# Weight sums of four stages' first units made in device memory ahead of time

## The chip, the cores and the metric

One core of one Trainium2 chip runs the whole program. The metric is the device time of one execution in microseconds (us); the time of a kernel is the median of its runs. For one execution there is a profile: which engine ran which instruction when, what each wait was released by, and what the sixteen DMA engines moved. Engines are named as the profile names them: PE multiplies matrices (PEld loads its weights), DVE and ACT work on elements, POOL is used here almost only to issue accumulating transfers, SP issues plain transfers.

## The reference

One layer of a streaming encoder on 512 frames of width 2048, all in 32-bit floats:

```python
h = rms_norm(x, norm_mix_w);  proj = h @ w_in        # split into two groups
y_a = banded softmax attention (16 heads);  y_g = gated linear attention (4 heads), norm, silu gate
x = x + concat([y_a, y_g]) @ w_out
u = causal_depthwise_conv(rms_norm(x, norm_ffn_w) @ w_ffn_up, w_ffn_conv, b_ffn_conv)
x = x + (gelu(u_gate) * u_val) @ w_ffn_down          # inner width 5632
x = x + sigmoid(rms_norm(x, norm_ple_w) @ w_ple_gate) * (p @ w_ple_proj)
return rms_norm(x, final_norm_w)
```

## The kernel before

The program has two halves. **The first**, up to some 320 us, projects values for the linear attention (`vproj`, lines 230 to 258: sixteen weight pages of 128 x 1024, two column halves of eight), then does the linear attention head by head (`gla_proj`, line 1110, and `gla_core`, line 1158), then projects values for the softmax attention (`values_a`, line 1036). A weight page comes by `wtile` (line 116): one DMA on SP into one of three raw pages, a rounded copy by ACT, the remainder by DVE, each into one of three pages more. In the second half of the value projection `input_pair` (line 1067) also writes the operands of the next stage to memory, seven pieces of 128 KB for each of eight pairs (line 276, all issued by SP).

**The second** is a list of stages, each a matrix product done by Winograd's form of the 2 x 2 block product: a unit is a pair of output blocks, and takes seven products of 24 matmuls (`product`, line 481) from seven weight pages: L11, L12, L22 are blocks of the weights, and S1 = L21 + L22, S2 = S1 + L11, S3 = L21 + L11, S4 = S2 + L12 are sums of blocks. The order of the products is P1, P2, P6, P5, P7, P3, P4, with pages L11, L12, S2, S1, S3, S4, L22. Stages run in the order `pp`, `in` (query, key and gate projections with softmax attention beside them), `pp`, `wo`, `up`, `dn0`, `dn1`, `dn2`, `pg`. In `wo`, `up`, `dn0` to `dn2` and `pg` the first two and the last two units run as pairs, product by product in turn.

How a unit gets its sums is set by a word, `sums`. For `"dma"`, the word of the first and last pairs of all stages here, SP loads L21 into two pages (line 406) and POOL adds L22 to the one and L11 to the other by accumulating DMAs (line 407), which gives S1 and S3; DVE makes S2 into a page of its own (line 431) and turns it into S4 in place (line 440). Pages come from a pool of nine (`free`, line 376), in the order of the list `wanted` (built on line 852 from `NEEDS`); `issue` (line 389) starts a load whenever a page is free, `used` (line 409) frees a page after its last use. Two steps before a product, `prep_high` makes sums and has ACT round the page (line 465); `prep_low` has DVE take the remainder (line 472). At a stage's start ACT and DVE also split the stage's operands, read back from memory (`load` on line 336 and `split` on line 342; the last two pieces come straight from the units before).

The order of the work has two sources. From the stages on, DVE, ACT and PE keep the program's order (`InOrder`, line 56, switched on at line 1277), and a hand-written `agenda` says at which step what is done. Everything else, and SP and POOL throughout, is ordered by the framework's scheduler when the program is built; each engine then runs its list strictly in that order, waiting where an instruction's inputs aren't there.

Of the kernel before, what the change touches and what calls it, by code (L numbers as in the profile page):

```python
# [12 lines left out]
ALU = mybir.AluOpType  # L13

P = 128
# [16 lines left out]
PLAIN = ("P1", "P2", "P6", "P5", "P7", "P3", "P4")  # L32
HALVES = ("P1", "P2", "P6", "P7", "P4", "P5", "P3")
# [8 lines left out]
def encoder_block(ctx: ExitStack, tc: tile.TileContext, A, out):  # L42
    nc = tc.nc
# [4 lines left out]
    pg = ctx.enter_context(tc.tile_pool(name="pages", bufs=1))  # L48
# [54 lines left out]
    late = []  # L103
# [107 lines left out]
    nmix, nffn, nple, nfin = (cols[:, i * KD:(i + 1) * KD] for i in range(4))  # L211
# [4 lines left out]
    first = xslot(0, "x0_0")  # L216
# [50 lines left out]
    def scratch(name, shape):  # L267
        return dp.tile(list(shape), F32, name=name)
# [36 lines left out]
    mixd = operand_scratch("mix", 8)  # L305
# [7 lines left out]

    class Stage:
        def __init__(self, name, units, kb, xd, weights, after, sums, edge, last=PLAIN, begin=None, begin_at=0,
                     chained=False, pace=None, late=(), single=False):
            self.name, self.kb, self.xd, self.weights, self.after = name, kb, xd, weights, after
            self.begin, self.begin_at, self.pace, self.late = begin, begin_at, pace, late
            self.chained, self.tail, self.quarter = chained, [None, None], None
            self.n = (4, kb - 4 - 2 * chained)  # L320
            self.x = {}
            n = len(units)
            self.units = [Unit(self, u, last if i >= n - 2 else PLAIN, edge if i < 2 or i >= n - 2 else sums)
                          for i, u in enumerate(units)]
            for i in range(n):
                self.units[i].pos = i
            if single:
                self.groups = [[u] for u in self.units]
                return
            self.units[0].first = True  # L330
            for i in range(2):
                self.units[i].head = i
                self.units[n - 2 + i].last = i
            self.groups = [self.units[:2]] + [[u] for u in self.units[2:-2]] + [self.units[-2:]]
# [7 lines left out]
        def split(self, op, g, body=True, tails=(0, 1)):  # L342
# [6 lines left out]
            if self.chained and g == 1:  # L349
# [4 lines left out]


    NEEDS = {"dma": ("L11", "L12", "S1", "S2*", "S3", "L22"), "dve": ("L11", "L12", "L21", "L22", "S1*", "S2*"),
             "s3": ("L11", "L12", "L21", "L22", "S1*", "S2*")}

    class Unit:
        def __init__(self, stage, u, order, sums):  # L360
            self.stage, self.u, self.order, self.sums = stage, u, order, sums
            self.first, self.head, self.last = False, None, None
            self.w, self.tag = {}, {}
            if sums == "dma":
                self.uses = dict(L11=2, L12=2, S1=2, S2=2, S3=1, L22=1)
                self.made = {"S2", "S4"}
            else:
                self.uses = dict(L11=3, L12=2, S1=2, S2=2, L21=2, L22=2)
                self.made = {"S1", "S2", "S3", "S4"}
            self.parts = dict(C11=2, C12=2, C22=2, C21=1)  # L370
            self.have = set()
            self.left = dict(A=4, B=1, C=2)
            self.o = None
            self.banks = {}
# [14 lines left out]
    def issue():  # L389
        kept, i = 0, 0  # L390
        while i < len(wanted):
            unit, name = wanted[i]
            if len(free) <= kept:
                return
            if name[-1] == "*":
                kept += 1
                i += 1
                continue
            wanted.pop(i)
            n = unit.stage.kb * P  # L400
            t = raw_page(unit, name)[:, :n]
            src = lambda q: unit.stage.weights(unit.u, q)
            if name[0] == "L":
                nc.sync.dma_start(t, src(name))
            else:
                nc.sync.dma_start(t, src("L21"))
                nc.gpsimd.dma_start(t, src("L22" if name == "S1" else "L11"), accum_op=ALU.add)  # L407

    def used(unit, name):
        unit.uses[name] -= 1  # L410
# [35 lines left out]
    def prep_high(i, own=None):  # L446
        if i >= len(steps):
            return None
        unit, prod = steps[i]
        name = PRODUCTS[prod][0]  # L450
        n = unit.stage.kb * P
        make(unit, name)
        if prod == unit.order[0] and unit.sums != "dma":
            make(unit, "S1")
        if i + 1 < len(steps):
            nxt, p = steps[i + 1]
            q = PRODUCTS[p][0]
            if (nxt is unit or nxt.paired) and (q != "S4" or "P6" in nxt.w):
                make(nxt, q)
        if i > 0 and steps[i - 1][1] == "P6" and steps[i - 1][0].paired:  # L460
            make(steps[i - 1][0], "S4")
        key = {"S4": "S2"}.get(name, "L21" if name == "S3" and unit.sums != "dma" else name)
        raw = unit.w[key]
        hi, lo = own or (page("wh", "wh", F32R), page("wl", "wl", F32R))
        act.activation(hi[:, :n], raw[:, :n], AF.Copy)
        unit.w[prod] = hi, lo
        return unit, key, hi[:, :n], lo[:, :n], raw[:, :n]
# [61 lines left out]
    streams = [x_in] + [scratch(f"x{i}d", (8, P, 2, T)) for i in range(1, 4)]  # L529
    h2d, h3d = operand_scratch("h2", 8), operand_scratch("h3", 8)  # L530
# [112 lines left out]
    def after_gate(unit):  # L643
# [5 lines left out]
                (3, 0, lambda: nc.sync.dma_start(x3d[unit.u], xs))] + squares(unit, 2)  # L649

    blk2 = lambda w: lambda m, q: w[m + 8 * (q[1] == "2"), int(q[2]) - 1]
    stages = [Stage("wo", list(range(8)), 8, mixd, blk2(A["w_out"]), after_norm(streams[1], h2d, nffn), "s3", "dma",
                    begin=lambda u: load_x(streams[0], u), begin_at=6, chained=True)]
    order, f0, slots = [], 0, {}
    for ci, n in enumerate(CHUNKS):
        for k in range(n // 2):
            for second in range(2):
                f = f0 + k + second * n // 2
# [1 line left out]
                slots[f] = (ci, k, second)  # L660
        f0 += n
    stages.append(Stage("up", order, 8, h2d, lambda f, q: A["w_up"][f + FB * (q[1] == "2"), int(q[2]) - 1], after_up,
                        "dma", "dma", chained=True, pace=(22, 5.8), late={-3: 2, -2: 6, -1: 12}))
    stages[0].quarter = last_quarter(lambda: stages[4], nffn)
    for u in stages[1].units:
        u.slot = slots[u.u]
# [163 lines left out]
    mids = streams[1:3] + [scratch("x2d_", (8, P, 2, T)), streams[3]]  # L830
    for ci, n in enumerate(CHUNKS):
        stages.append(Stage(f"dn{ci}", list(range(8)), n // 2, gd[ci], blk2(A[f"w_dn{ci}"]),
                            after_add(mids[ci + 1]) if ci < 2 else after_norm(streams[3], h3d, nple),
                            "dve", "dma", begin=lambda u, s=mids[ci]: load_x(s, u), begin_at=0 if ci else 8, late={}))
    stages.append(Stage("pg", list(range(8)), 8, h3d, blk2(A["w_ple_gate"]), after_gate, "dma", "dma", last=HALVES,
                        begin=load_gate, begin_at=9, chained=True, pace=(15, 5.3), late={}))
    stages[4].quarter = last_quarter(lambda: stages[8], nple)

    stages[0].tail = tails
# [65 lines left out]
    def more_banks():  # L905
        aux_tags[:] = ["b6", "b7"]
        banks.extend(("b4", "b5"))

    agenda[base[front.units[7]] + 7 + 12].append((5, attention_done))
    agenda[i0 + 9].append((0, more_banks))  # L910
    for st in stages:
# [124 lines left out]
    def values_a(c, between=None, then=None):  # L1036
        def place(t):
            vstage[c, t] = xslot(4 * c + t, "va")
            return vstage[c, t]

        vproj(A["w_v_a"], c, place, between=between, then=then)
        for t in range(TT):
            (nc.scalar if c else nc.sync).dma_start(vad[4 * c:4 * c + 4, :, t].rearrange("b p v -> p b v"),
                              vstage[c, t].rearrange("p (b v) -> p b v", b=4))
# [3 lines left out]
    with ExitStack() as mix:  # L1048
        vp = mix.enter_context(tc.tile_pool(name="v", bufs=1, side="right"))

        with ExitStack() as gctx:
# [106 lines left out]
            def gla_core(hd, eb, en, dd, dec2):  # L1158
# [60 lines left out]
                for vb in range(2):  # L1219
                    nc.vector.scalar_tensor_tensor(o[vb], o[vb], gnw[:, vb:vb + 1], rg, ALU.mult, ALU.mult)  # L1220
                    nc.sync.dma_start(ond[hd][:, vb], o[vb])

            st = gla_proj(0)
            for hd in range(1, 4):
                nxt = gla_proj(hd)
                gla_core(hd - 1, *st)
                st = nxt
            values_a(0)
            gla_core(3, *st)

    xa.append(ctx.enter_context(tc.tile_pool(name="xa", bufs=1, side="right", reuse_waits="tile")))
# [283 lines left out]
```

## Time and profile before

| | us |
|---|---|
| median of 3 runs | 2297.38 |
| lowest, highest | 2296.74, 2305.6 |
| the profiled execution | 2290.98 |
| its span, from the first to the last instruction | 2289.3 |

The page of the profile gives the busy time of each engine, the DMA queues (q1 is fed by SP, q0 by POOL) and the chain of work that ended last. Beside it the trace answers questions: the timeline of one engine in a stretch, the busy times of all engines in chosen stretches, groups of like instructions. A row of a timeline reads: start, duration, engine, line, operation, what is written from what, count, and in brackets the idle time before it with what ended it. L64 is the helper behind `vec`, `act` and `ten`, so there the names of the tiles tell the rows apart: `wh` and `wl` are the rounded page and the remainder, `l` a loaded weight page, `s` a page of sums, `wo_R`, `up_R` and so on operands, `acc` accumulators.

### The profile page before, as it was taken

Reading aid. Unit: us, or ns where it says so; the run is one execution under the profiler, and the core shown is the slowest. Engines: PE = TensorE matmul, PEld = TensorE weight load, DVE = VectorE, ACT = ScalarE, POOL = GpSimd, SP = SyncE. Lnnn points to the kernel's source line nnn. Section 1 sums busy time; section 2 is a strip of 40 time slices with the busy share of each in tenths; the row PEclk is TensorE's granted clock in tenths of the full one; section 3 lists DMA queues with packets and bytes.
Section 4 is the critical chain, followed back from the end, with each engine's and each line's share of the span. In section 5 each row is a group of like instructions: output and inputs, shape, how many; then the busy total and the mean of one; then the engine's idle time right before and its main releaser. Section 6 shows DMA issues by size and latency. Waiting matters only on the chain.

```text
span 2289.3 us, 44978 instructions
## 1 busy us (share of the span) xinstructions
PE 2255.1 (99%) x18004; PEld 2183.3 (95%) x18004; DVE 1885.3 (82%) x2587; ACT 1302.1 (57%) x1913; POOL 143.6 (6%) x181
## 2 busy tenths in 40 slices
PE   9999999999999999999999999999999999999997
PEld 8888889999999999999999999999999999999997
DVE  7566369998788888998888888888898787998987
ACT  6354357776665665555555555555564554656656
POOL 0000000000000100000000000010000100001000
PEclk9999999999999999999999999999999999999998
DMA  6623596666978977787877777777866967879895
GB/s 218 206 74 104 179 283 171 184 183 200 316 252 258 326 215 212 203 223 205 222 199 222 213 216 208 216 212 214 254 212 230 314 219 241 300 242 330 273 289 191
DMA packets 195570, 516.78 MB, mean 226 GB/s; under 512 B 20928, under 2 KB 72384, under 8 KB 195360
## 3 DMA queue, kind: packets, MB, share of 16 engines
q1 hardware_dynamic: 167168, 423.42, 52.8%
q0 software_dynamic: 23616, 84.95, 21.1%
q10 hardware_dynamic: 4576, 5.54, 0.7%
q8 instruction: 141, 2.31, 0.4%
q14 instruction: 69, 0.57, 0.1%
HBM read 435.18 MB, written 76.55 MB: 224 GB/s over the span
## 4 chain that ended last, share of the span: by engine, by line
PE 84%; DVE 7%; DMA 4%; ACT 3%; issue 2%; ACTq 0%; DVEq 0%; SPq 0%; POOLq 0%
PE accA L64 39%; PE accC L64 20%; PE accB L64 10%; PE v L252 3%; PE v L254 3%; PE v L253 3%; DVE wl L64 2%; DMA l<-in_w_dn 1%; DVE s L64 1%; DMA s<-in_w_dn 1%; PE py L64 1%; PE ptr L64 1%; PE psc L64 1%; DMA wo_T<-mix_T 1%; DMA s<-in_w_blk 1%
## 5 line engine op out<-in xcount | busy, mean ns | idle before, releaser
L64 DVE TENSOR_TENSOR wl<-s,wh 128x1024 fp32r<-128x1024 f32 (+1 forms) x365 | 437.5, 1199 | 62.8 <-ACT wh L64 61.7
L64 ACT ACTIVATE wh<-l 128x1024 fp32r<-128x1024 f32 (+1 forms) x308 | 319.2, 1037 | 184.8 <-PE accC L64 117.2
L64 DVE TENSOR_TENSOR wl<-l,wh 128x1024 fp32r<-128x1024 f32 (+1 forms) x308 | 367.6, 1194 | 56.8 <-ACT wh L64 56.4
L64 ACT ACTIVATE wh<-s 128x1024 fp32r<-128x1024 f32 (+1 forms) x365 | 377.9, 1036 | 34.8 <-DVE s L64 18.5
L64 ACT ACTIVATE u<-accA 128x256 f32<-128x256 f32 x290 | 109.4, 377 | 363.8 <-PE accA L64 363.7
L64 DVE TENSOR_TENSOR s<-s,l 128x1024 f32<-128x1024 f32 (+1 forms) x192 | 229.5, 1195 | 9.4 <-DMA s<-in_w_blk 9.2
L64 PE MATMUL accA<-up_T,wh 128*128 128x256 f32 x1408 | 178.9, 279 | 0.1
L64 PEld LDWEIGHTS accA<-up_T,wh 128*128 128x128 f32 x1408 | 170.6, 188 | 0.3 <-ACT wh L64 0.3
L64 DVE SCALAR_TENSOR_TENSOR cv<-u,cw,cv 128x511 f32<-128x511 f32 (+1 forms) x176 | 131.5, 747 | 3.1
L407 POOL DMA_DIRECT2D s<-in_w_up x88 | 75.1, 853 | 788.3 <-DMA s<-in_w_up 360.6
L252 PE MATMUL v<-wv_h,h 128*128 128x512 f32 x256 | 100.2, 391 | 0.4 <-ACT h L153 0.4
L254 PE MATMUL v<-wv_h,h 128*128 128x512 f32 x256 | 100.2, 391 | 0.0
L253 PE MATMUL v<-wv_l,h 128*128 128x512 f32 x256 | 99.7, 389 | 0.0
L64 PE MATMUL accA<-up_T,wl 128*128 128x256 f32 x704 | 96.5, 279 | 0.0
L64 PE MATMUL accB<-up_R,wh 128*128 128x256 f32 x704 | 90.5, 280 | 2.0 <-DVE up_R L64 1.3
L64 PE MATMUL accA<-dn_T,wh 128*128 128x256 f32 x704 | 90.4, 280 | 1.9 <-ACT wh L64 1.9
L64 PE MATMUL accA<-up_R,wh 128*128 128x256 f32 x704 | 89.7, 279 | 0.0
L64 PE MATMUL accC<-up_N,wh 128*128 128x256 f32 x704 | 89.3, 279 | 0.0
L64 PE MATMUL accC<-up_R,wh 128*128 128x256 f32 x704 | 89.3, 279 | 0.0
L64 PE MATMUL accA<-up_N,wh 128*128 128x256 f32 x704 | 89.3, 279 | 0.0
L64 PEld LDWEIGHTS accA<-up_T,wl 128*128 128x128 f32 x704 | 88.5, 188 | 0.0
L64 PEld LDWEIGHTS accB<-up_R,wh 128*128 128x128 f32 x704 | 85.7, 188 | 2.7 <-DVE up_R L64 1.5
(402 smaller groups left out, 5060.0 us busy)
## 6 DMA issues: line engine op xcount, KB each, us to landing
l<-in_w_up SPq DMA_DIRECT2D x132, 512.0 KB, 5.4
s<-in_w_up SPq DMA_DIRECT2D x88, 512.0 KB, 4.7
s<-in_w_up POOLq DMA_DIRECT2D x88, 512.0 KB, 6.3
l<-in_w_dn SPq DMA_DIRECT2D x56, 448.0 KB, 5.2
l<-in_w_blk SPq DMA_DIRECT2D x36, 512.0 KB, 4.5
l<-in_w_out SPq DMA_DIRECT2D x28, 512.0 KB, 4.9
l<-in_w_dn SPq DMA_DIRECT2D x28, 512.0 KB, 5.6
s<-in_w_blk SPq DMA_DIRECT2D x24, 512.0 KB, 4.6
```

What stands on the lines that cost most here:

```text
L64: ins = f(*args, **kw)
L252: nc.tensor.matmul(ps[t], h1[kt][:, 0, sl], wh, start=kt == 0, stop=False)
L253: nc.tensor.matmul(ps[t], h1[kt][:, 0, sl], wl, start=False, stop=False)
L254: nc.tensor.matmul(ps[t], h1[kt][:, 1, sl], wh, start=False, stop=kt == KD - 1)
L407: nc.gpsimd.dma_start(t, src("L22" if name == "S1" else "L11"), accum_op=ALU.add)
```

## The change

A third word, `"memory"`, for the first two units of `wo`, `up`, `dn0` and `pg`: eight units. For each, four pages in device memory (rows of 1152 floats apart, 1024 used) take the sums. `sum_begin` copies L21 into two of them, L11 and L12 into the others, by plain DMAs on SP from memory to memory; `sum_add` then makes S1 (+ L22), S3 (+ L11), S2 (+ S1) and S4 (+ S2) by accumulating DMAs on POOL from memory to memory. The calls for six units stand between the heads of the linear attention, those for the two of `pg` at five steps of the stage `in`. When the stages come, all seven pages of such a unit are loaded as they are by SP, each into a page of its own that is free again after one use. The unit then needs no addition on DVE and no accumulating DMA. All other units are as before.

```diff
+            how = [first or edge] * 2 + [sums] * (n - 4) + [edge] * 2
...
+             "memory": ("L11", "L12", "S2", "S1", "S3", "S4", "L22"),
...
+            if sums == "memory":
+                self.uses = dict.fromkeys(NEEDS[sums], 1)
+                self.made = set()
...
             if name[0] == "L":
                 nc.sync.dma_start(t, src(name))
+            elif unit.sums == "memory":
+                nc.sync.dma_start(t, sumd[unit, name])
...
+    def sum_begin(unit):
+        src = lambda q: unit.stage.weights(unit.u, q)
+        for name, q in (("S1", "L21"), ("S3", "L21"), ("S2", "L11"), ("S4", "L12")):
+            sumd[unit, name] = scratch(f"{unit.stage.name}{unit.u}_{name}", (P, 1152))[:, :unit.stage.kb * P]
+            nc.sync.dma_start(sumd[unit, name], src(q))
+
+    def sum_add(unit, *names):
+        for name in names:
+            q = {"S1": "L22", "S3": "L11", "S2": "S1", "S4": "S2"}[name]
+            nc.gpsimd.dma_start(sumd[unit, name], sumd[unit, q] if q[0] == "S" else unit.stage.weights(unit.u, q),
+                                accum_op=ALU.add)
+
+    def sum_step(us, i):
+        if i < len(us):
+            sum_begin(us[i])
+        for back, names in ((1, ("S1", "S3")), (2, ("S2",)), (3, ("S4",))):
+            if 0 <= i - back < len(us):
+                sum_add(us[i - back], *names)
...
+    for i in range(5):
+        agenda[base[front.units[2 + i]]].append((0, lambda i=i: sum_step(summed[6:], i)))
...
+            sum_step(summed[:6], 0)
             st = gla_proj(0)
+            sum_step(summed[:6], 1)
             for hd in range(1, 4):
                 nxt = gla_proj(hd)
+                sum_step(summed[:6], 2 * hd)
                 gla_core(hd - 1, *st)
+                sum_step(summed[:6], 2 * hd + 1)
                 st = nxt
             values_a(0)
+            sum_step(summed[:6], 8)
             gla_core(3, *st)
```

More of the change, by code (lines that the diff above doesn't have):

```diff
@@ L315, in __init__ @@
         def __init__(self, name, units, kb, xd, weights, after, sums, edge, last=PLAIN, begin=None, begin_at=0,
-                     chained=False, pace=None, late=(), single=False):
+                     chained=False, pace=None, late=(), single=False, first=None):
             self.name, self.kb, self.xd, self.weights, self.after = name, kb, xd, weights, after
@@ L322, in __init__ @@
             n = len(units)
-            self.units = [Unit(self, u, last if i >= n - 2 else PLAIN, edge if i < 2 or i >= n - 2 else sums)
+            how = [first or edge] * 2 + [sums] * (n - 4) + [edge] * 2
+            self.units = [Unit(self, u, last if i >= n - 2 else PLAIN, how[i])
                           for i, u in enumerate(units)]
@@ L363, in __init__ @@
             self.w, self.tag = {}, {}
-            if sums == "dma":
+            if sums == "memory":
+                self.uses = dict.fromkeys(NEEDS[sums], 1)
+                self.made = set()
+            elif sums == "dma":
                 self.uses = dict(L11=2, L12=2, S1=2, S2=2, S3=1, L22=1)
@@ L407, in issue @@
                 nc.gpsimd.dma_start(t, src("L22" if name == "S1" else "L11"), accum_op=ALU.add)
+    sumd = {}
+    def sum_begin(unit):
[14 more added lines that the diff above has]
+                sum_add(us[i - back], *names)
     def used(unit, name):
@@ L452, in prep_high @@
         make(unit, name)
-        if prod == unit.order[0] and unit.sums != "dma":
+        if prod == unit.order[0] and unit.sums in ("dve", "s3"):
             make(unit, "S1")
@@ L461, in prep_high @@
             make(steps[i - 1][0], "S4")
-        key = {"S4": "S2"}.get(name, "L21" if name == "S3" and unit.sums != "dma" else name)
+        key = name
+        if unit.sums != "memory":
+            key = {"S4": "S2"}.get(name, "L21" if name == "S3" and unit.sums != "dma" else name)
         raw = unit.w[key]
@@ L651, in encoder_block @@
     blk2 = lambda w: lambda m, q: w[m + 8 * (q[1] == "2"), int(q[2]) - 1]
-    stages = [Stage("wo", list(range(8)), 8, mixd, blk2(A["w_out"]), after_norm(streams[1], h2d, nffn), "s3", "dma",
+    stages = [Stage("wo", list(range(8)), 8, mixd, blk2(A["w_out"]), after_norm(streams[1], h2d, nffn), "s3", "dma", first="memory",
                     begin=lambda u: load_x(streams[0], u), begin_at=6, chained=True)]
@@ L662, in encoder_block @@
     stages.append(Stage("up", order, 8, h2d, lambda f, q: A["w_up"][f + FB * (q[1] == "2"), int(q[2]) - 1], after_up,
-                        "dma", "dma", chained=True, pace=(22, 5.8), late={-3: 2, -2: 6, -1: 12}))
+                        "dma", "dma", first="memory", chained=True, pace=(22, 5.8), late={-3: 2, -2: 6, -1: 12}))
     stages[0].quarter = last_quarter(lambda: stages[4], nffn)
@@ L833, in encoder_block @@
                             after_add(mids[ci + 1]) if ci < 2 else after_norm(streams[3], h3d, nple),
-                            "dve", "dma", begin=lambda u, s=mids[ci]: load_x(s, u), begin_at=0 if ci else 8, late={}))
-    stages.append(Stage("pg", list(range(8)), 8, h3d, blk2(A["w_ple_gate"]), after_gate, "dma", "dma", last=HALVES,
+                            "dve", "dma", begin=lambda u, s=mids[ci]: load_x(s, u), begin_at=0 if ci else 8, late={},
+                            first=None if ci else "memory"))
+    stages.append(Stage("pg", list(range(8)), 8, h3d, blk2(A["w_ple_gate"]), after_gate, "dma", "dma", last=HALVES, first="memory",
                         begin=load_gate, begin_at=9, chained=True, pace=(15, 5.3), late={}))
+    summed = [u for st in stages for u in st.units if u.sums == "memory"]
     stages[4].quarter = last_quarter(lambda: stages[8], nple)
```

## The prediction

> **What bounds the kernel now.** I began with the page's head and its queues, since the change moves work from DVE to the DMA engines.
>
> ```profile
> span 2289.3 us, 44978 instructions
> PE 2255.1 (99%) x18004; PEld 2183.3 (95%) x18004; DVE 1885.3 (82%) x2587; ACT 1302.1 (57%) x1913; POOL 143.6 (6%) x181
> ...
> q1 hardware_dynamic: 167168, 423.42, 52.8%
> q0 software_dynamic: 23616, 84.95, 21.1%
> ```
>
> PE is the bound: outside a few places it has no gap, so DVE time saved there is worth nothing, and a PE stall anywhere is paid in full. The places where PE does wait are the stage starts. In the chain of work a product of 24 matmuls takes 2.80 us; the timeline of PE shows where the first pair of a stage begins and a product that comes late.
>
> ```profile
> 684.30 2.80 PE accA L64 x24
> ...
> 634.30 2.03 PE L64 MATMUL accA<-wo_R,wh 128*128 128x256 f32 x16
> 656.00 2.03 PE L64 MATMUL accC<-wo_N,wh 128*128 128x256 f32 x16
> ...
> 796.14 2.03 PE L64 MATMUL accA<-up_R,wh 128*128 128x256 f32 x16
> 807.69 2.03 PE L64 MATMUL accB<-up_R,wh 128*128 128x256 f32 x16
> ...
> 1664.60 2.03 PE L64 MATMUL accA<-dn_R,wh 128*128 128x256 f32 x16
> 1695.78 2.03 PE L64 MATMUL accC<-dn_R,wh 128*128 128x256 f32 x16
> ...
> 2103.04 2.04 PE L64 MATMUL accA<-pg_R,wh 128*128 128x256 f32 x16
> 2120.32 2.03 PE L64 MATMUL accA<-pg_N,wh 128*128 128x256 f32 x16
> ```
>
> Between the two rows of each stage lie 6, 3, 10 and 4 products, 16.80, 8.40, 28.00 and 11.20 us at 2.80. They took 21.70, 11.55, 31.18 and 17.28. So `wo` loses 4.90 us, `up` 3.15, `dn0` 3.18, `pg` 6.08: 17.3 us in all, the most that this change can win there.
>
> **What goes: sums on DVE.** Each pair loses four additions. The timeline of DVE shows three of `wo`'s inside its stall, and in `up` and `pg` one ahead of the split that PE waits for; `dn0`'s first comes well ahead of its stall.
>
> ```profile
> 644.00 1.22 DVE L64 TENSOR_TENSOR s<-s,l 128x1024 f32<-128x1024 f32 x1
> 645.14 1.22 DVE L64 TENSOR_TENSOR wl<-l,wh 128x1024 fp32r<-128x1024 f32 x1
> ...
> 648.35 1.21 DVE L64 TENSOR_TENSOR s<-s,l 128x1024 f32<-128x1024 f32 x1
> ...
> 652.22 1.21 DVE L64 TENSOR_TENSOR s<-s,l 128x1024 f32<-128x1024 f32 x1
> ...
> 802.51 1.22 DVE L64 TENSOR_TENSOR s<-s,l 128x1024 f32<-128x1024 f32 x1
> 805.12 0.68 DVE L64 TENSOR_TENSOR up_R<-up_R 128x512 fp32r<-128x512 f32 x1
> ...
> 1668.44 1.22 DVE L64 TENSOR_TENSOR s<-s,l 128x1024 f32<-128x1024 f32 x1
> ...
> 2110.96 1.22 DVE L64 TENSOR_TENSOR s<-s,l 128x1024 f32<-128x1024 f32 x1
> 2113.56 0.68 DVE L64 TENSOR_TENSOR pg_R<-pg_R 128x512 fp32r<-128x512 f32 x1
> ```
>
> One addition holds DVE for 1.14 us (644.00 to 645.14). `wo`: DVE works without a gap there, so three of them are 3.4 us. `up` and `pg`: one each, 1.1, and then ACT, which makes the rounded half of the same split, is the last to come. `dn0`: four, 4.6, of which at most the loss of 3.2 can be had. Sum 3.4 + 1.1 + 3.2 + 1.1 = **8.8 us**; bounds 0 (ACT or a load takes the place everywhere) and 17.3 (all four losses go). Accumulating DMAs go from these starts too, four a pair. A transfer of 512 KB (0.524 MB) holds all sixteen DMA engines for 0.528 x 2289.3 / (423.42 / 0.524) = 1.50 us on q1, and 0.211 x 2289.3 / (84.95 / 0.524) = 2.98 on q0. A pair loses four of 2.98 on q0 and keeps q1's bytes and four more pages (the sums DVE had made): 10 loads and 4 accumulates, 26.9 us, become 14 loads, 21.0. That helps the late operands; I count it within the bounds, not in the sum. SP issues four more loads a pair, at some 0.4 us each, with nothing urgent behind them that pages don't hold anyway. Each page is free after one use, so prefetch gets no shallower: nothing.
>
> **What comes: 32 copies and 32 accumulates.** By the two prices, 32 x 1.50 = 48 us and 32 x 2.98 = 95 us, 143 us of all DMA engines. Memory to memory is in no row; I take these rows for want of nearer ones. Bounds: accumulates at the plain price, 48 + 48 = 96; both twice as dear, 286. Whether this is free depends on when it runs. The views that decide are the timelines of SP and ACT, then DMA share by stretches.
>
> ```profile
> 26.11 0.43 SPq L903 DMA_DIRECT2D cw<-in_conv  x1
> 31.15 16.26 SPq L125 DMA_DIRECT2D wv_r<-in_w_v_g  x4
> ...
> 69.67 0.40 SPq L125 DMA_DIRECT2D wv_r<-in_w_v_g  x1
> ...
> 18.36 0.29 ACT L1105 ACTIVATE ones_r<-ones 128x128 fp32r<-128x128 f32 x1
> ...
> 74.31 1.06 ACT L126 ACTIVATE wv_h<-wv_r 128x1024 fp32r<-128x1024 f32 x1 [10.32 <-DMA wv_r<-in_w_v_g]
> 81.36 1.06 ACT L126 ACTIVATE wv_h<-wv_r 128x1024 fp32r<-128x1024 f32 x1 [5.99 <-DMA wv_r<-in_w_v_g]
> 85.64 1.06 ACT L126 ACTIVATE wv_h<-wv_r 128x1024 fp32r<-128x1024 f32 x1 [3.21 <-DMA wv_r<-in_w_v_g]
> ...
> 26.00:50.00 24.00, 24.00 (x111) 19.78 (x109) 14.14 (x25) 11.74 (x16) 0.00 (x0) 1.00 0.37 117
> 50.00:88.00 38.00, 38.00 (x168) 31.33 (x167) 28.68 (x54) 8.77 (x11) 0.52 (x1) 1.00 0.77 239
> 88.00:110.00 22.00, 21.96 (x96) 17.76 (x96) 6.89 (x8) 11.22 (x15) 0.00 (x0) 1.00 0.48 153
> 110.00:200.00 90.00, 89.91 (x445) 74.87 (x444) 57.73 (x91) 49.43 (x64) 0.00 (x0) 1.00 0.24 77
> 200.00:285.00 85.00, 84.90 (x423) 70.74 (x422) 40.06 (x51) 30.39 (x36) 0.00 (x0) 1.00 0.49 160
> ...
> 293.56 1.00 POOL L407 DMA_DIRECT2D s<-in_w_blk  x1 [216.30 <-DMA s<-in_w_blk]
> ```
>
> The first row is the one to stop at. Line 903 loads the convolution's taps and stands in `attention_done`, in the program behind the whole linear attention and most of stage `in`; SP issued it at 26 us, between two weight loads. It needs nothing but its own tile, so the scheduler put it where SP's list first had a hole. The row of line 1105 says the same of ACT: written behind the value projection, done at 18.36. The 32 copies need nothing either: they read inputs and write fresh memory. So I expect **all copies to begin at about 26 us**, in the value projection, wherever `sum_step` is written, and the accumulates, which wait only for copies and for each other, to follow at once on POOL, idle until 293.56.
>
> There the DMA engines aren't idle. From 26 to 110 us they are busy 24 x 0.37 + 38 x 0.77 + 22 x 0.48 = 48.7 of 84 us: 35 are free. And PE has little in hand: the pages loaded from 69.67 on are already awaited by ACT for 10.32, 5.99 and 3.21 us, that is ACT works each on arrival. A copy queued on SP ahead of such a load delays it by its own time, and an accumulate shares the engines with both. From 110 to 285 us 90 x 0.76 + 85 x 0.51 = 112 us are free.
>
> I take it that half of both kinds runs before 110 us (the 128 KB stores and the loads come first in SP's list whenever they are ready, and S2 and S4 wait for others): 24 + 48 = 72 us against 35 free, **37 us late**. The other half, 71 us, fits into the 112 behind it: nothing. If none is in the way, 0; if all of it, 143 - 35 = 108. POOL blocks behind an accumulate whose copy hasn't landed; queued behind it are a memset of the gate's page (line 1077) and, from 293.56 on, the first accumulates of stage `in`. With 71 us of work in 112 us free these should still be met; if not, some us at 300 more.
>
> Two rules of the Trainium skill bear on this. DMA: Bandwidth & Descriptors, in the section on queues, rings and completion order, says that each DMA engine takes the rings it has work for in turn, packet by packet. No row here shows the turns. By it alone a load would get one packet for each accumulate's, 1.50 of every 4.48 us while both queues have work, so that a page takes 4.5 us, and every copy ahead of it as long; the sum of 37 then counts as a middle, not a ceiling. The same page, in the section on the anatomy of a DMA on the gpsimd path, prices such a DMA at 2.0 us plus its bytes by 436 GB/s, which for 512 KB is an estimate of 1.2 us of movement. The trace disagrees with 2.98 us of engine time; by the page's figure the accumulates would be cheap, which is the third case below.
>
> **The sum** against the execution of 2290.98 us: + 37 - 9 = 2319. Its time lies 6.4 us under the median of the runs shown, 2297.38, so the forecast is 2297.4 + 28.2, about **2326 us**.
>
> **The rivals.**
> - *The copies stay where they are written*, two units a head from some 90 us on. For it: only one load on SP shows the early placing. Against: it shows it on the very queue, and ACT too. Then 24 copies and 24 accumulates, 36 + 72 = 107 us, meet 11 + 68 + 43 = 122 free us from 88 to 285, pages that are read every few us have three raw pages in reserve, and nothing is late: 2297.4 - 8.8 = 2288.6, in bounds 2280 to 2297. This is the case on the other side. It turns at the point where the copies issued before 70 us, with what they start, pass the 24 x 0.63 + 20 x 0.23 = 20 free us there.
> - *They go early, but cheaply*: accumulates cost the engines 1.50, like plain transfers. Then 24 + 24 = 48 us against 35, 13 late, less 8.8: 2301.6. For it: both move the same bytes. Against: 2.98 in the queues' rows.
> - *The gain doesn't come*: at the starts ACT and the loads of operands come last, and the sums on DVE were beside them. With early copies 2334, without 2297. `pg` and `up`, where ACT's half is needed first, speak for it, `wo` against.
>
> **How the numbers follow.** Early and dear: 0.63, with or without the gain, 2310 to 2400 (at twice the price or with all work in the way it ends near 2397). In place: 0.25, of which 0.12 win more than the 11.5 us that are 0.5%, since the transfers freed at the starts come on top. Early but cheap: 0.12, nearly all within 0.5%. This gives faster 0.14, same 0.23, slower 0.63; 0.5% is about what a measurement of this kernel can tell from no change. The range leaves out the best of the second case (0.06) and the dearest of the first (0.1): 2284 to 2385. The likeliest case's own range is 2310 to 2385.
>
> **What would show it.** In the timeline of SP, line by line: the new copies between 26 and 60 us (right) or from 88 us on (the first rival). In the windows from 26 to 110 us: DMA share near 1.0, fewer matmuls of PE than 111, 168 and 96, and ACT waiting for loads of `wv_r` far longer than 10 us. In the queues: 16 more accumulates on q0 than before (32 new, 16 gone), at 2.98 us each or not. At the stage starts: no `s<-s,l` on DVE, 656.00 - 634.30 shrunk from 21.70 to about 18.3, `dn0` from 31.18 to 28, `up` and `pg` by 1.1 each; if these stay, the step on the gain was wrong. The forecast falls if PE keeps its matmul counts up to 285 us.

## The result, and the profile after

The changed kernel takes 2340.82 us, median of 6 runs (2327.16 to 2343.93), beside 2301.01 us (2296.16 to 2306.91, 6 runs) for the kernel before on the same chip: ratio 1.0164, 95% interval 1.0142 to 1.0185. By the ratio it is 38 us slower; the forecast of 2326 lay 28.6 above the median that it started from. The profiled execution took 2334.74 us with a span of 2333.0. Both profiled executions lie below their medians (before by some 10 us, after by 6), so differences between the two traces come out a few us larger than the difference of the medians.

The head of the page and its two big queues:

```profile
span 2333.0 us, 45053 instructions
...
PE 2271.6 (97%) x18004; PEld 2197.8 (94%) x18004; DVE 1871.3 (80%) x2571; ACT 1302.4 (56%) x1913; POOL 158.2 (7%) x197
...
q1 hardware_dynamic: 174080, 448.59, 54.6%
q0 software_dynamic: 25920, 93.33, 22.9%
```

DVE is busy for 14 us less, as meant, and q0 carries 93.33 MB in the place of 84.95, which is 16 pages of 0.524 MB: 32 new accumulates, 16 gone. PE has the same 18004 matmuls and fell from 99% to 97% of a longer span.

Where the time went is read at marks that PE passes in both traces. The timeline of PE, first matmul of the first product of `in`, in the kernel before:

```profile
319.14 2.03 PE L64 MATMUL accA<-in_R,wh 128*128 128x256 f32 x16
```

and after, with the first and a later product of the four stage starts (the same products as in the prediction):

```profile
362.62 2.03 PE L64 MATMUL accA<-in_R,wh 128*128 128x256 f32 x16
...
681.42 2.03 PE L64 MATMUL accA<-wo_R,wh 128*128 128x256 f32 x16
699.09 2.04 PE L64 MATMUL accC<-wo_N,wh 128*128 128x256 f32 x16
...
840.43 2.04 PE L64 MATMUL accA<-up_R,wh 128*128 128x256 f32 x16
850.73 2.03 PE L64 MATMUL accB<-up_R,wh 128*128 128x256 f32 x16
...
1714.08 2.05 PE L64 MATMUL accA<-dn_R,wh 128*128 128x256 f32 x16
1742.35 2.05 PE L64 MATMUL accC<-dn_R,wh 128*128 128x256 f32 x16
...
2148.01 2.03 PE L64 MATMUL accA<-pg_R,wh 128*128 128x256 f32 x16
2163.97 2.05 PE L64 MATMUL accA<-pg_N,wh 128*128 128x256 f32 x16
```

At the first product of `in` PE is 43.5 us late: the whole loss stands ahead of 363 us. The starts gave something back: `wo` took 17.67 us in the place of 21.70, `up` 10.30 for 11.55, `dn0` 28.27 for 31.18, `pg` 15.96 for 17.28, together 9.5 us. The difference at the end is 43.7 all the same. `in` took 3.6 us more than before, `wo` behind its start 1.2 and `up` behind its start 6.4, where most products took 2.83 us in this execution and 2.80 in that of before; `dn0` to `dn2` behind the start took 1.6 less. None of the sums in memory is made in these stretches, and the same stages differ by nearly as much between traces of kernels in which they are alike (last section).

Now the stretch that lost. SP's timeline, the copies (L423) among the loads of value weights (L125):

```profile
26.16 1.24 SPq L423 DMA_DIRECT2D wo_S<-in_w_out  x2
...
47.92 1.14 SPq L423 DMA_DIRECT2D up_S<-in_w_up  x2
93.08 0.41 SPq L125 DMA_DIRECT2D wv_r<-in_w_v_g  x1
...
111.25 0.52 SPq L423 DMA_DIRECT2D up_S<-in_w_up  x1
...
168.19 4.89 SPq L423 DMA_DIRECT2D pg_S<-in_w_ple_gate  x2
```

The first copy goes out where the taps `cw` went before, at 26 us. But only 11 copies are out by 50 us; the other 21 stand behind the stores of h1 and the last value weights, from 111 to 173 us. The load of `wv_r` that went out at 69.67 before goes out at 93.08. The busy times by stretches (PE with its matmuls first, then PEld, DVE, ACT, POOL, the granted clock, the DMA engines' share, GB/s):

```profile
26.00:50.00 24.00, 24.00 (x111) 19.96 (x110) 14.20 (x25) 11.83 (x17) 2.64 (x3) 1.00 0.96 285
50.00:88.00 38.00, 31.92 (x129) 25.24 (x127) 15.60 (x30) 5.59 (x8) 6.60 (x8) 0.91 1.04 272
88.00:110.00 22.00, 10.76 (x39) 8.46 (x40) 12.63 (x25) 3.35 (x4) 0.52 (x1) 0.77 0.91 274
110.00:200.00 90.00, 71.90 (x329) 59.26 (x328) 36.68 (x52) 31.72 (x42) 13.14 (x16) 0.89 1.02 296
200.00:285.00 85.00, 84.89 (x420) 69.92 (x419) 51.30 (x76) 42.22 (x52) 4.15 (x5) 1.00 0.48 131
```

and in ACT's timeline the wait for the first load that comes late:

```profile
97.67 1.06 ACT L126 ACTIVATE wv_h<-wv_r 128x1024 fp32r<-128x1024 f32 x1 [33.24 <-DMA wv_r<-in_w_v_g]
```

Read the DMA share first: 0.96, 1.04, 0.91, 1.02. From 26 to 200 us the engines are busy for 24 x 0.96 + 38 x 1.04 + 22 x 0.91 + 90 x 1.02 = 174 of 174 us (a share over 1 means that packets overlap). PE lost 39 matmuls to 88 us, 57 to 110 and 116 to 200: 212 at some 0.2 us each (90 us by 445 in `before`), 43 us. In `before`, PE had the 608 matmuls that it has here at 200 us by about 157 us, and for them the engines worked 8.9 + 29.3 + 10.6 + 0.24 x 47 = 60 us. The other 114 are the sums.

The linear attention shows the same from the side of its loads. The medians from issue to landing between 88 and 200 us, before:

```profile
wkg_r<-in_w_blk SPq DMA_DIRECT2D x8, 512.0 KB, 3.5
wqg_r<-in_w_blk SPq DMA_DIRECT2D x8, 512.0 KB, 3.4
```

and after:

```profile
wkg_r<-in_w_blk SPq DMA_DIRECT2D x8, 512.0 KB, 13.0
wqg_r<-in_w_blk SPq DMA_DIRECT2D x6, 512.0 KB, 17.4
```

and the longest piece of the chain of waits there, in the changed kernel:

```profile
166.58 21.62 DMA wqg_r<-in_w_blk
```

A page that came in 3.4 us takes up to 21.62. PE runs out of work at 171.92 and starts again at 189.89, once this page is there and split: these are the 18 us that it lost between 110 and 200.

### The profile page after: what moved, and what is told of

The parts are those of the page before. It is cut to its first block, busy times and chain, and to the rows that moved or that the text cites. A ratio compares the mean times of both kernels' runs of the same rounds, so it can differ in the third digit from the quotient of the medians.

```text
span 2333.0 us, 45053 instructions
## 1 busy us (share of the span) xinstructions
PE 2271.6 (97%) x18004; PEld 2197.8 (94%) x18004; DVE 1871.3 (80%) x2571; ACT 1302.4 (56%) x1913; POOL 158.2 (7%) x197
## 3 DMA queue, kind: packets, MB, share of 16 engines
q0 software_dynamic: 25920, 93.33, 22.9%
## 4 chain that ended last, share of the span: by engine, by line
PE 84%; DMA 6%; DVE 6%; ACT 2%; issue 2%; SPq 0%; DVEq 0%; POOL 0%; ACTq 0%; POOLq 0%
PE accA L64 40%; PE accC L64 20%; PE accB L64 10%; PE v L253 2%; PE v L252 2%; PE v L254 2%; DMA wqg_r<-in_w_blk 2%; DVE wl L64 1%; DMA s<-in_w_blk 1%; PE pp L64 1%; PE py L64 1%; PE ptr L64 1%; PE psc L64 1%; DMA h_R<-pair_r 1%; DVE u L64 1%
## 5 line engine op out<-in xcount | busy, mean ns | idle before, releaser
L64 ACT ACTIVATE wh<-l 128x1024 fp32r<-128x1024 f32 (+1 forms) x308 | 319.6, 1038 | 188.3 <-PE accC L64 117.9
L64 DVE TENSOR_TENSOR s<-s,l 128x1024 f32<-128x1024 f32 (+1 forms) x176 | 210.3, 1195 | 9.4 <-DMA s<-in_w_blk 9.4
L64 DVE TENSOR_TENSOR u<-u,accC 128x256 f32<-128x256 f32 x98 | 41.0, 418 | 58.9 <-PE accC L64 57.9
```

The costliest lines, as they stand in the source:

```text
L64: ins = f(*args, **kw)
```

## The experiments

The theory after the result: sums of weights, above all their accumulates, fill the DMA engines while the value projection and the linear attention need their loads at once; the gain at the starts is real and comes from DVE. The rivals: the copies on SP's queue are the cost; the transfers cost the same wherever they run; the gain at the starts comes from the freed accumulates. Ratios are to the kernel before on the same chip, whose medians lay between 2299.4 and 2303.5 us; 0.1% is 2.3 us. The start of the first product of `in`, 319.14 before, tells the loss ahead of `in` without the noise of the rest; where none is given it lies between 319.2 and 319.8.

**The gain alone.**

```diff
-                nc.sync.dma_start(t, sumd[unit, name])
+                nc.sync.dma_start(t, src({"S1": "L21", "S3": "L21", "S2": "L11", "S4": "L12"}[name]))
...
     def sum_step(us, i):
+        return
```

> Makes no sums at all: the first pairs of the four stages load plain weight blocks in the place of S1 to S4 (so those products use wrong weights), with the same number of pages and no accumulating DMA. It is the change without its price. My theory: the four stage starts give back what the trace of the changed kernel shows, 4.0 at wo, 1.3 at up, 3.2 at dn0 and 1.3 at pg, so about 10 us under the kernel before, 2291. Rival, the gain is only seen because these stages start later beside other work: 2297 to 2301, no change. Rival, the making in memory only moved the loss and more than 10 is to be had: down to 2284.

2292.81 us, ratio 0.9955 (0.9939 to 0.9970): 10.4 us faster by the ratio. The theory's number; the starts' gain is a real one and the rival without a gain falls.

**The cost alone.**

```diff
-            how = [first or edge] * 2 + [sums] * (n - 4) + [edge] * 2
+            self.first = first
+            how = [edge] * 2 + [sums] * (n - 4) + [edge] * 2
...
-    summed = [u for st in stages for u in st.units if u.sums == "memory"]
+    summed = [u for st in stages if st.first for u in st.units[:2]]
```

> Makes all 32 sums in memory as the change does, but nobody reads them: the four stages begin as in the kernel before. It is the price of the change without its gain. My theory: the price is paid ahead of the stage in, by the value projection and the linear attention starved of the DMA engines, about 46 us, so 2347 (more than the changed kernel by about 10). Rival, part of the 40 us comes from the later loads of the plain pages at the stage starts: then 2320 to 2335.

2347.20 us, ratio 1.0202 (1.0173 to 1.0231): 46 us slower, with the first product of `in` at 363.30. 44.2 us of the price are paid ahead of `in`, whether or not anybody reads the sums.

**Copies without accumulates.**

```diff
-        for back, names in ((1, ("S1", "S3")), (2, ("S2",)), (3, ("S4",))):
-            if 0 <= i - back < len(us):
-                sum_add(us[i - back], *names)
```

> Makes the 32 copies and leaves out the 32 accumulates, so the pages hold one block in the place of a sum. 48 us of DMA engines by the queues' rows in the place of 143. My theory, the time is lost where the engines have no free time left: copies alone fill about 24 us against 35 free before 110 us, a few us late for those that stand on SP ahead of a load, less the 10 of the starts: 2295 to 2305. Rival, the copies' place on SP's queue ahead of the loads and stores is what costs, and accumulates run beside: about 2335. Rival, only accumulates cost: 2291.

2291.19 us, ratio 0.9940 (0.9918 to 0.9963). The timeline of PE:

```profile
319.32 2.03 PE L64 MATMUL accA<-in_R,wh 128*128 128x256 f32 x16
```

and the busy times in the stretch that the changed kernel lost first:

```profile
50.00:88.00 38.00, 38.00 (x168) 31.25 (x168) 28.27 (x54) 8.76 (x11) 0.52 (x1) 1.00 0.82 270
```

All matmuls of before are there, and `in` begins at 319.32. The 32 copies, where the scheduler put them on SP among the loads, cost nothing by themselves. The price comes with POOL's 32 transfers: of this run's rivals, "only accumulates cost" holds.

**Everything, pinned in its place.**

```diff
-            nc.sync.dma_start(sumd[unit, name], src(q))
+            tc.keep_in_program_order(nc.sync.dma_start(sumd[unit, name], src(q)))
```

> The whole change, with each copy pinned on SP behind what is traced before it, so that the first copy comes behind the last load of the value projection (about 90 us) and the copies stay where they are written; the accumulates follow by their data. My theory, it is the early placing that costs: PE keeps its matmuls up to 88 us, the linear attention has the free engines for the first two thirds, and what is left over is a few us: 2291 to 2300. Rival, 143 us more of DMA engines ahead of the stage in cost the same wherever they stand: about 2340.

2333.07 us, ratio 1.0137 (1.0113 to 1.0161): still 31.5 us slower. My theory said 2291 to 2300 and is wrong in this. The first products of `in` and of `wo` in PE's timeline:

```profile
346.87 2.03 PE L64 MATMUL accA<-in_R,wh 128*128 128x256 f32 x16
678.62 2.03 PE L64 MATMUL accA<-wo_R,wh 128*128 128x256 f32 x16
```

two stretches of its busy times:

```profile
50.00:88.00 38.00, 38.00 (x169) 31.25 (x168) 28.04 (x54) 8.76 (x11) 0.52 (x1) 1.00 0.74 238
...
110.00:200.00 90.00, 77.13 (x360) 63.74 (x361) 48.06 (x73) 39.03 (x49) 13.20 (x16) 0.92 1.00 267
```

and its queues from 88 to 200 us (packets, MB, share of the stretch):

```profile
q1 hardware_dynamic: 5923, 20.35, 51.3%
q0 software_dynamic: 2730, 9.96, 48.9%
```

The value projection is whole again (169 matmuls), and the linear attention pays: 27.7 us late at `in`. `in` itself, where the sums of `pg` stand four at a time, takes 331.8 us in the place of 315.2; in the twelve traces with no accumulate of these sums there it took 314.8 to 319.6. In these 112 us q0 held the engines for 54.8 us with 9.96 MB, 19 accumulates at 2.88; q1 for 57.5 with 38.8 pages at 1.48. On paper the 107 us of sums fitted into the 122 that were free up to 285 us before. But they came in a burst: by 200 us 19 accumulates and 20 copies, some 83 us, had gone through where 79 were free, with a DMA share of 1.00 and the loads late. So it isn't the early placing as such. Wherever they stand in a burst, the sums go through at the engines' full rate, and the loads that PE needs next wait among them.

**Plain transfers in the place of accumulates.**

```diff
-            nc.gpsimd.dma_start(sumd[unit, name], ..., accum_op=ALU.add)
+            nc.gpsimd.dma_start(sumd[unit, name], ...)
```

> The changed kernel with the accumulation switched off in the 32 transfers of POOL: they stay on the same queue, at the same places, with the same bytes, and overwrite in the place of adding (so the pages hold one block, not a sum). The copies alone cost nothing, so the accumulates are the price; this asks what of them is dear. My theory, the adding: an accumulate holds the engines 2.9 us, a plain transfer 1.4, so 32 x 1.4 = 45 us in the place of 93, about what the 112 us behind the value projection and the 35 in it leave free: 2292 to 2305. Rival, the path through POOL's queue is as dear with or without the adding, or the loads suffer from the second queue as such: 2330 to 2340.

2307.26 us, ratio 1.0023 (1.0003 to 1.0044), `in` begins at 340.94. From 110 to 200 us its q0 reads

```profile
q0 software_dynamic: 2994, 10.89, 34.7%
```

which is 31.2 us for 20.8 pages, 1.50 each, half of an accumulate. The adding doubles the price of a page, and POOL's transfers at half the price lose half of the time ahead of `in` (21.8 us in the place of 43.5). A bit above my 2305.

**Where the gain is from.**

```diff
-                nc.gpsimd.dma_start(t, src("L22" if name == "S1" else "L11"), accum_op=ALU.add)
+                if not (unit.stage.first and unit.pos < 2):
+                    nc.gpsimd.dma_start(t, src("L22" if name == "S1" else "L11"), accum_op=ALU.add)
```

> Makes no sums in memory. The four first pairs begin as before, with the additions on DVE, and only their accumulating DMAs (four a pair) are left out, so that S1 and S3 hold one block (wrong weights there). It parts the gain of 9 us into DVE's part and the DMA engines' part. My prediction's step, the additions on DVE are the loss: no gain, 2299 to 2302. Rival, the freed accumulates are the gain, as the operands come earlier: 2292.

2295.65 us, ratio 0.9981 (0.9961 to 1.0002): 4.4 us faster, with an interval from 9 to none, between the two theories. The timeline of PE is sharper:

```profile
634.51 2.03 PE L64 MATMUL accA<-wo_R,wh 128*128 128x256 f32 x16
654.48 2.03 PE L64 MATMUL accC<-wo_N,wh 128*128 128x256 f32 x16
...
1663.11 2.03 PE L64 MATMUL accA<-dn_R,wh 128*128 128x256 f32 x16
1694.29 2.05 PE L64 MATMUL accC<-dn_R,wh 128*128 128x256 f32 x16
```

`wo` takes 19.97 us, 1.7 less than before; `dn0` 31.18, as before to the last digit; `up` 11.58 and `pg` 17.47, as before. So of the 9.5 us at the starts about 1.7 come from the freed accumulates and the rest from DVE.

**Eight sums at the worst place.** Only `wo` keeps `first="memory"`; the other three stages begin as before.

> Only the 8 sums of wo, placed as early as in the changed kernel (copies from 26 us on); up, dn0 and pg begin as before. A quarter of the work at its worst place: 12 + 23 = 35 us of DMA engines against 35 free from 26 to 110 us. My theory, the loss begins where the free time ends, so 0 to 5 us late, less 4 at wo: 2297 to 2302. Rival, each accumulate delays the loads beside it whatever is free: a quarter of 46, 11.5 late, less 4: 2308.

2312.06 us, ratio 1.0046 (1.0025 to 1.0066): 10.6 us slower, with a quarter of the sums. The rival's number is nearer than mine. The timelines of PE and of DVE:

```profile
333.45 2.03 PE L64 MATMUL accA<-in_R,wh 128*128 128x256 f32 x16
```

```profile
67.46 0.76 DVE L64 TENSOR_TENSOR tp<-pair_r 128x256 f32<-128x256 f32 x2 [8.46 <-DMA h_T<-tp]
```

14.3 us are lost ahead of `in`. The accumulates went out from 32 to 71 us and had landed by 79. Until then before had 24 x 0.63 + 29 x 0.23 = 21.8 us free, not the 35 up to 110 us: 12 + 23 = 35 less 21.8 is 13.2. The 79 is read from this run's own trace, so the sum explains the loss afterwards and no further run tests it. The last row offers another reason: DVE waits for a store of h1 to land before it can write `tp` again, and SP, the loads behind it, waits for DVE. The next two runs put that to the test.

**A chain through the stores, or throughput?** Five sets of buffers for those stores in the place of two, with `wo`'s sums early, and alone.

```diff
-                store_pair(h1d, k, ..., gp.tile([P, 1024], F32, tag="tp", name="tp", bufs=2))
+                tag = ("tp", "tp", "eb", "en", "dd")[k % 5]
+                ...
+                store_pair(h1d, k, ..., t)
```

> The kernel with the 8 sums of wo alone made early, which came out 10.6 us slower than the kernel before, with one more edit: the stores of h1's derived blocks take five sets of buffers in turn (the two of tp, and three made of the tags eb, en and dd, which stand empty until the linear attention) in the place of two. Theory A, a chain: accumulates stretch the landing of the 128 KB stores from 1.9 to 4 us and over, DVE waits for a free tp, SP for DVE's next block, and the weight loads behind the stores on SP come late; with five sets DVE and SP run through, so most of the 14.6 us of loss goes: 2297 to 2303. Theory B, throughput: 35 us of sums do not fit into the free time whatever the order of the waits, so 2310 to 2314.

> The control for that run: the kernel before with the five sets of buffers and no sums in memory at all. Both theories: PE has no gap there before, so no change, 2299 to 2303. Should it be faster, the five sets help by themselves and the run above is read against this one.

2308.81 us, ratio 1.0041 (1.0023 to 1.0060), and alone 2300.55 us, ratio 1.0009 (0.9986 to 1.0031). The chain through the buffers falls: DVE no longer waits there, yet `in` begins at 333.13, as late as with two. SP's timeline, and its waits from 50 to 70 us (us in total, times, longest), say why:

```profile
51.99 1.46 SPq L276 DMA_DIRECT2D h_R<-pair_r  x3
...
59.51 6.39 SPq L276 DMA_DIRECT2D h_R<-pair_r  x3
```

```profile
SPq L276 <- DMA h_R<-pair_r: 6.2, 3, 2.8
...
SPq L276 <- DMA wv_r<-in_w_v_g: 3.1, 1, 3.1
```

Three issues that take 1.46 us take 6.39 while the accumulates run, though their data are there: SP waits for earlier transfers of its own. In this program SP's transfers tell of their landing on eight semaphores, taken in turn, and in none of the 14 traces does one go out before the transfer eight ahead of it has landed. These three go out at 59.51, 62.46 and 65.58; the landings that they wait for stand at 59.49, 62.39 and 65.56. So at most eight are on their way, slow landings hold up every issue behind them, and the next load of `wv_r` goes out at 83.69 in the place of 69.67. Throughput, theory B, is right by the number, 0.41% slower beside 0.46% with two sets; the late loads come by a chain all the same, through SP's eight transfers, which neither theory named.

**Sums late, one at a time.** `sum_one` makes one page, copy and accumulate, at one place.

```diff
+    def sum_one(unit, name):
+        ...
+        tc.keep_in_program_order(nc.sync.dma_start(t, src(a)))
+        nc.gpsimd.dma_start(t, sumd[unit, b] if b[0] == "S" else src(b), accum_op=ALU.add)
...
+        agenda[base[stages[4].units[4 + 2 * i]]].append((0, lambda u=u, name=name: sum_one(u, name)))
```

> Only the 16 sums of dn0 and pg, made one at a time during the stage up, one every second unit (about 39 us apart), the copies pinned on SP there; wo and up begin as in the kernel before. My theory, an accumulate costs nothing where the loads have pages in reserve and the engines have about 9 us free between two sums, each of which takes 1.5 + 2.9: no loss ahead, the gain of dn0 and pg, 3.2 + 1.3, stays: 2296 to 2298. Rival, an accumulate costs PE about 1.4 us wherever it runs (45 us by 32): 2301 - 4.5 + 22 = 2319.

2295.49 us, ratio 0.9970 (0.9953 to 0.9987): 7 us faster. In the stretch with the 16 sums PE has no gap:

```profile
840.00:1660.00 820.00, 820.00 (x6962) 819.52 (x6961) 707.00 (x838) 433.87 (x586) 83.45 (x98) 1.00 0.84 232
```

The same operations cost nothing here. The rival of a fixed price for each accumulate falls.

**The version that beats both: `wo`'s sums in the attention's value projection.** As the last, and in addition

```diff
-            values_a(0)
+            values_a(0, lambda kp: sum_one(summed[kp // 4], ("S1", "S3", "S2", "S4")[kp % 4]))
```

> The sums of dn0 and pg made one at a time in the stage up, as in the run that came out 7 us faster, and in addition the 8 sums of wo, one behind each of the first eight weight pages of the value projection of the attention (about 200 to 270 us), copies pinned on SP there; up begins as before. My theory: in that stretch ACT waits for PE and not for the loads (the pages are 4.4 us ahead), and a sum of 1.4 + 2.9 us stands against 3.9 free us for a page, so no loss there and wo's gain of 4 on top: 2290 to 2293. Rival, each accumulate ahead of the stage in delays PE by what it did in the early placing, 14.6 us by 8: 2308.

2289.04 us (12 runs, before 2300.18), ratio 0.9951 (0.9932 to 0.9969): 11 us faster than the kernel before, and by the intervals as fast as the gain alone without any making. PE's timeline, and the busy times in the stretch in which six of the 8 accumulates went out (two went ahead of it):

```profile
635.30 2.03 PE L64 MATMUL accA<-wo_R,wh 128*128 128x256 f32 x16
652.86 2.04 PE L64 MATMUL accC<-wo_N,wh 128*128 128x256 f32 x16
```

```profile
200.00:285.00 85.00, 84.93 (x423) 70.76 (x422) 41.10 (x55) 31.41 (x37) 4.90 (x6) 1.00 0.76 234
```

DMA share is 0.76 where it was 0.49, PE keeps its 423 matmuls, and `wo`'s start takes 17.56 us.

**The same eight sums in the stage `in`,** one at a unit.

> As the run with the sums of wo in the value projection of the attention (0.9951 of the kernel before), but these 8 sums stand in the stage in, one at a unit (about 24 us apart), copies pinned on SP. In the run with all copies pinned where they are written, the 8 sums of pg stood in the same stage, four copies and four accumulates at a time, and PE lost 10 us from 400 to 500 us. My theory, it was the bunching: the engines have about 6.7 us free for each unit there, a sum takes 4.3, so no loss: 2289 to 2292. Rival, the stage in has no reserve against any accumulate, about 1.3 us of PE for each: 2300.

2294.09 us, ratio 0.9968 (0.9951 to 0.9984): 7 us faster, between theory and rival, and by the intervals not told apart from the last. The trace has a price: `in` begins at 319.55 and `wo` at

```profile
641.25 2.03 PE L64 MATMUL accA<-wo_R,wh 128*128 128x256 f32 x16
```

so `in` took 321.7 us in the place of 315.2. Without any accumulate of these sums there it took up to 319.6 in other traces, so of the 6.5 us between 2.1 and all may be the price of the 8 sums; one trace doesn't tell, and neither does it tell whether spacing alone is enough there.

## Why the prediction was right or wrong

**Copies go early: right in kind.** The first copy went out at 26.16, in the hole where `cw` had shown it. That all would be on their way by 60 us was wrong: 11 were, and 21 stood behind the stores.

**The prices: right.** 1.50 and 2.98 us were taken from loads into SBUF. Memory to memory an accumulate is 2.88; copies and loads together are 1.48 in the pinned run, and the copies alone some 1.38 in the run that makes nothing else (q1's share from 26 to 200 us rose from 40.1 to 65.4%, 44 us for 32). The rival "early but cheap" had 1.50 for an accumulate; that is what a transfer without the adding costs, and with it the kernel came out at 2307.26, near that case's 2301.6. The Trainium skill's page DMA: Bandwidth & Descriptors, section Anatomy of one DMA — SWDGE (gpsimd) path, by which 512 KB is an estimate of 1.2 us of movement, disagrees with 2.88; the transfer without the adding, 1.50, is nearer to it.

**37 us: nearly the right size, by luck: two mistakes cancel.** The step took half of the work, 72 us, before 110 us. It was 11 copies and 11 accumulates, 16 + 32 = 48, which by the step's rule is 13 us late against 35 free; PE was 96 matmuls, 20 us, late by then. And the step failed on the second half: "The other half, 71 us, fits into the 112 behind it: nothing." It cost 116 matmuls, some 23 us, by 200 us. The engines' free time there is no place for it, since the loads of the linear attention are issued when they are needed and the sums stand in the queues at the same time. Free time counts only up to the moment when the load behind it is due, and only if the sums come slowly enough to leave it. The run with 8 sums fits the first part of that rule, 13.2 by the sum and 14.3 in the trace. So 43.5 came in the place of 37.

**POOL's queue, "some us at 300 more": no.** The last sum's accumulate went out at 223.66, and the first one of `in` behind it.

**The gain: right in size and cause.** 8.8 was said; the trace has 9.5 at the four starts, and the run without the making gave 10.4 (6.9 to 14.0). `wo` came to 17.67, said about 18.3; `dn0` to 28.27, said 28; `up` and `pg` gained 1.25 and 1.32, said 1.1 each. The freed accumulates, kept within the bounds, are 1.7 of it at `wo`. The rival without a gain falls.

**The rival on the other side: wrongly priced.** Copies in their written place were given 2288.6 and a chance of 0.25. The run that pins them took 2333.07. Had the scheduler left them there, the kernel would have been slower as well, so faster and same had too much weight. The error is the one above: 107 us of work against 122 free, with no question when either is due. Its point of turning, copies ahead of 70 us, isn't one.

**The rule of turns: not refuted.** The Trainium skill's page DMA: Bandwidth & Descriptors, section Queues, rings and completion order, has each engine take its rings in turn, packet by packet; by it a page would take 4.5 us beside accumulates, and every copy ahead of it as long. The trace agrees where accumulates land: between 168 and 180 us pages of SP's queue landed at 168.18, 172.57, 176.36 and 179.95, and accumulates at 172.07, 175.98 and 179.99, one for one. Where none landed, pages came at 162.19, 163.36, 164.80, 166.50 and 168.18. The load of 166.58 stood behind seven pages that SP had issued ahead of it, so its 21.62 us are eight landings. The 13.0 and 17.4 are of this kind, and not the 4.5 of a load that goes out alone. How much of the loss is the engines' share and how much the place behind SP's own transfers stays open: no run gives the loads a queue of their own.

**The end.** 43.5 of loss less 9.5 of gain is 34; the medians differ by 39.8, the ratio says 32.7 to 42.6. The range held it.

## What to carry to other kernels

Free DMA time isn't a store to draw on: ask for each stretch when its next load is due, how many pages it has in reserve, and how much extra work stands in the queues, its own included, at that moment. The 32 sums cost 46 us in a burst among loads on demand; 24 of them cost nothing one at a time where pages lay ready. An operation that depends on nothing goes where the scheduler finds a hole; its written place means nothing unless it is pinned or waits for data.

## What the runs showed of the hardware

PE is slow for a while behind a wait. After the 11 us that it waited in the changed kernel, matmuls of 512 columns start 0.43 us apart up to 102.8, four us behind the first, and 0.23 apart from then on:

```profile
98.78 0.80 PE L252 MATMUL v<-wv_h,h 128*128 128x512 f32 x1 [11.01 <-ACT wv_h L126]
...
101.91 0.63 PE L254 MATMUL v<-wv_h,h 128*128 128x512 f32 x1
102.33 0.63 PE L252 MATMUL v<-wv_h,h 128*128 128x512 f32 x1
...
103.34 0.39 PE L252 MATMUL v<-wv_h,h 128*128 128x512 f32 x1
103.57 0.39 PE L253 MATMUL v<-wv_l,h 128*128 128x512 f32 x1
```

So a wait costs more than its length: of the 43 us, 35.3 are idle (6.1, 11.2 and 18.1 in the three stretches, less 0.1 of before) and 8 are matmuls at the lower clock of 0.77 to 0.91 in the rows of the stretches. The Trainium skill's page TensorE: Matmul & The Clock Gate, Part 1 on the clock gate, says that the clock is halved after an idle window and full again after some 3.4 us of work. The trace agrees, with 0.43 by 0.23 and four us.

In stretches where PE has no gap and a granted clock of 1.00, a product of 24 matmuls took 2.80 us in one execution and 2.83 in another of the same stage, for hundreds of us at a time. From the first product of `up` to that of `dn0` the kernel before took 868.5 us, and the kernel with five sets of buffers and no sums in memory, in which `up` is the same, 876.3. These 8 us are not much less than the 10.8 between the fastest and the slowest of the six runs before. No run tells the cause.
